# Stage sums behind the next projection, weight transfers later and products in pairs: a hybrid decoder layer on one core of a Trainium2 chip

## The chip, the cores and the metric

The kernel runs on one core of one Trainium2 chip. The metric is the device time of one launch in microseconds. Inputs and outputs lie in the chip's memory; the host only lays the inputs out before the launch.

## What is computed

One layer with two sub-layers, for a sequence of 2048 tokens of width 1024. The part of the reference that matters:

```python
mod = (silu(c) @ w_ada + b_ada)                       # 6 vectors of 1024
sh1, sc1, g1, sh2, sc2, g2 = split(mod, 6)
h = x * (1 + sc1) + sh1
z = h @ w_in                                          # (2048, 1024) @ (1024, 2048)
gate_b, gate_c, v_conv, v_pool = split(z, 4)
y_conv = gate_b * short_conv(gate_c * v_conv, conv_w)  # causal, width 3
y_pool = multiscale_pool(v_pool, w_pool, pool_scale)   # windows 2, 4, 8, 16
mix = concat([y_conv, y_pool]) @ w_out                # (2048, 1024) @ (1024, 1024)
x = layer_norm(alpha * x + (1 + g1) * mix, ln1_g, ln1_b)
h = x * (1 + sc2) + sh2
f = square(relu(h @ w_mlp_in)) @ w_mlp_out            # 1024 -> 4096 -> 1024
x = layer_norm(alpha * x + (1 + g2) * f, ln2_g, ln2_b)
```

All of it is float32.

## The kernel before

**A triple product.** TensorE multiplies in a rounded form of float32. Each operand is split into a high part (a copy in the rounded type, made by ScalarE, L145) and a low part (the operand less its high part, made by VectorE, L146), and `mm3` (L151 to L159) issues three matmuls for one product of tiles: high by high (L152), high by low (L153) and low by high (L154).

**Fewer products.** The large matrix products are cut into 2 by 2 blocks (in the down projection into 4 by 4), and sums of blocks are multiplied instead of the blocks: seven products take the place of eight in the three projections ahead, and the down projection is done in 26 products of such sums. The sums of operands are additions on VectorE (`tt`, L162), and the results are put together by additions out of PSUM.

**Order of the work.** The sequence is done in two halves of 1024 tokens, b = 0 and b = 1. For each half come the input projection (`in_proj_0`, then `in_proj_1` for the second half, four groups of channels), the output projection with the first layer norm (`out_proj`), and the up projection (`first_map`, which runs `up` for g = 0 to 7, eight groups of 512 hidden columns). When both halves are done, `down` computes the down projection for all tokens, and `Close` does the second layer norm and stores the result. Each engine has its own queue and works in order. Which instruction comes next on each queue is set when the kernel is built: the planner takes instructions by the order in which the program names them, but passes over one that would still have to wait in its model. A tile is drawn from a ring of a fixed number of buffers (`o` 10, `r` 5, `w` 6, `h` 28, PSUM banks `ps` 8, `mv` 8), and the next user of a buffer waits for the last reader.

**The up projection's sums.** `up` (L1068) makes four blocks (`c11`, `c12`, `c21`, `c22`) out of seven products, squares them, and then makes sums of them for the down projection, in four stages listed in `U_SUMS`: 3, 7, 13 and 10 additions of 128x256. Sums are stored to `usum` by POOL's DMA queue. For the last group of the first half (`late`), the stages 2 and 3 are put on a list, `owed`. `flush` runs what is on the list. In the kernel before, `flush` is called behind the last product of `up` (L1175, stage 2) and behind product 0 of the next input projection's first group (L744, stage 3).

**The next projection's start.** `group(0)` of `in_proj_1` (L736) runs products 0 to 6 in order. Behind product 0 it copies the banks out (`keep`, ScalarE L730), behind product 1 it adds (`add`, VectorE, from PSUM). Between them `inputs` loads and splits the operands that later products need.

**Transfers beside products.** `sums_down` (L1183) yields 80 DMA transfers of 512 KB, chip memory to chip memory, that make sums of down-projection weights (`wsum`), on POOL's queue; half of them add to what is there. They are tied to products: `mm3` counts its calls while the second half runs (the beats), and at each beat in `W_BEATS` it issues the next transfer, which waits for that product's last matmul. The input projection has the beats 1 to 224, the output projection 225 to 336, the up projection 337 to 784.

**The down projection.** `PRODUCTS` lists 26 products: the slot of `usum`, the weight blocks that are added (most often one or two), a sign, whether new banks are begun, and which results (row block t, column half d) read them. A product that begins no new banks goes on in those of two products before. `operand` loads and splits the operands of a step (a product and a quarter of its depth), four steps ahead. The first two products run their first three quarters before the fourth. When a result has been read for the last time, `finish` multiplies by the gate and adds the residual, and `Close.normalise` follows when both halves of its rows are done. `mv` tiles hold the statistics of rows.

**The gate row.** Beside the second half's up projection, `second_side` runs one job at each of nine beats of its own (`timed`; there are seven to a group from group 1 on, and beat 34 is behind product 0 of group 6). A job runs to its first yield at its beat, and on three beats later. Eight jobs load a column block and form a dot product; the ninth, `gate_row`, adds the bias (L277), then turns eight columns into a row with a transpose on TensorE (L225), a copy on ScalarE (L226) and two DMAs.

**The start of the up projection.** `turned` (L843) stores parts of its operands to `hsave` and loads them again (L880, L895) for sums (`back`). `out_proj` stores normalised rows to `nsave` (L990), on POOL's queue.

Of the kernel before, what the change touches and what calls it, by code (L numbers as in the profile page):

```python
# [27 lines left out]
WINDOWS = (2, 4, 8, 16)  # L28
HALO = 16
Q = 256  # L30
W_BEATS = {*range(48, 200, 7), *range(336, 752, 7)}
QUARTERS = slice(0, 256), slice(256, 512)

SLOTS = 26
# [28 lines left out]
)  # L63
W_KEPT = 18
PRODUCTS = (
# [26 lines left out]
)  # L92
# [15 lines left out]
def tile_hybrid_layer(ctx: ExitStack, tc: tile.TileContext, opening, xT, x, wada, win,  # L108
# [612 lines left out]
    def in_proj_1(X, W, first_w):  # L721
        mixed = []
        ops = Operands(mixed)

        def cut(rows_, h):
            return [r[:, o + h * H : o + h * H + H] for r, o in rows_]

        def keep(dst, banks):
            for p in range(2):
                nc.scalar.copy(dst[p], banks[p])  # L730

        def add(dst, banks):
            for p in range(2):
                tt(dst[p], dst[p], banks[p], ALU.add)

        def group(j):  # L736
            x_, y_, z_ = {}, {}, {}
            ready = W if j == 0 else block_weights(wins[j])
            product = seven(ready, X, None if j else first_w)
            v, u = t_o(WW), t_o(WW)  # L740
            values = (v, HALO), (u, 2)
            product(0, x_, True)
            keep(cut(values, 0), x_)
            flush()  # L744
            nc.vector.tensor_copy(v[:, :HALO], vhalo[:, j, :])
            nc.vector.tensor_copy(u[:, :2], uhalo[:, j, :])
            if j == 0:
                inputs(X, ORDER[3][1])
            product(1, y_, True)
            add(cut(values, 0), y_)  # L750
            if j == 0:
                inputs(X, ORDER[4][1])
            yield
            gc, gb = t_o(), t_o()
            gates = (gc, 0), (gb, 0)
            last = j == NG - 1
            product(2, x_, False)
            keep(cut(values, 1), x_)
            if j == 0:
                inputs(X, ORDER[5][1])  # L760
            product(3, z_, True)
            keep(cut(gates, 1), z_)
            if j == 0:
                inputs(X, ORDER[6][1])
            if last:
                ops.begin(0)
            yield
            product(4, x_, False)
            add(cut(gates, 1), x_)
            if last:  # L770
                ops.begin(1)
            product(5, z_, False)
            add(cut(values, 1), z_)
            if last:
                ops.weights(0, 1)
                pt = pool_mid(1, j, v)
            product(6, x_, False)
            keep(cut(gates, 0), x_)
            if last:
                ops.weights(1, 1)  # L780
                ops.second(0)
            yield
            if not last:
                pt = pool_mid(1, j, v)
            y = gc
            for hs in halves if last else [slice(0, T)]:
                w = hs.stop - hs.start
                tt(u[:, 2 + hs.start : 2 + hs.stop], u[:, 2 + hs.start : 2 + hs.stop], gc[:, hs], ALU.mult)
                conv(j, u[:, hs.start : hs.stop + 2], y[:, hs], w)
                tt(y[:, hs], y[:, hs], gb[:, hs], ALU.mult)  # L790
                if last and hs.start == 0:
                    mixed.extend([y[:, :H], None, pt[:, :H], pt[:, H:]])
                    ops.third(0)
                    ops.third(1)
            sums = mixed_sums(y, pt, u, v)
            if last:
                mixed[1] = sums[0]
                mixed.extend(sums[1:])
            else:
                store_mixed(j, y, pt, u, v)  # L800

        groups = [group(j) for j in range(NG)]
        for _ in range(3):
            next(groups[0])

        for j in range(1, NG):
            last = j == NG - 1
            next(groups[j])
            if not last:
                next(groups[j])  # L810
            next(groups[j - 1], None)
            if last:
                next(groups[j])
            next(groups[j])
        next(groups[-1], None)
        return ops
# [9 lines left out]
        return root  # L826

    def whole_stats(st):
        mv = mk(sm, [P, 8], F32, "mv", 8)
        nc.vector.bn_aggr(mv[:, 0:2], st.rearrange("p a b -> p (a b)"))  # L830
        return mv

# [117 lines left out]
    def out_proj(b, ops):  # L950
# [27 lines left out]

        def end(t, cs, other, scalar=1.0):
            if t not in mv:  # L980
                mv[t] = mk(sm, [P, 8], F32, "mv", 8)
            i = 4 + cs.start // H
            begun[:] = [nc.vector.scalar_tensor_tensor(R[t][:, cs], R[t][:, cs], scalar, other, op0=ALU.mult,
                                                       op1=ALU.add, accum_out=mv[t][:, i : i + 1]).ins]
# [75 lines left out]

    owed = []

    def flush():
        while owed:
            made_of, stage = owed.pop(0)
            made_of(stage)

    def up(b, g, B, beside, turn):  # L1068
# [103 lines left out]
            mark[0] = nc.scalar.activation(c21[:, ps[p]], X[p], AF.Relu).ins  # L1172
        nc.scalar.activation(c21, c21, AF.Square)
        made(c21, 1, 0)
        flush()  # L1175
        if late:
            owed.append((sums, 3))
        else:
# [161 lines left out]
    class Close:  # L1340
# [34 lines left out]
        def add(self, t, cs, ps):  # L1375
# [2 lines left out]
                self.added = tt(F[:, cs], F[:, cs], ps, ALU.add)  # L1378
                return
            if t not in self.mv:  # L1380
                self.mv[t] = mk(sm, [P, 8], F32, "mv", 8)
            i = 4 + cs.start // H
            self.added = nc.vector.scalar_tensor_tensor(F[:, cs], F[:, cs], 1.0, ps, op0=ALU.mult, op1=ALU.add,
                                                        accum_out=self.mv[t][:, i : i + 1])
# [44 lines left out]
        dot(f, r)  # L1429

    def gate_row():
        yield
        biased(G2, G2 + KD)
        g2 = mk(sm, [P, D], F32, "bc", 1)
        row_by_dram(g2, mod[:, G2 : G2 + KD], 1)
        gate.append(g2)

# [13 lines left out]

    def second_side():
        rows_ = [gate_dot(f) for f in range(G2, G2 + KD)] + [gate_row()]
        return timed(dict(zip((4, 6, 11, 13, 18, 20, 25, 27, 31), rows_)))

    gate = []

# [90 lines left out]
```

## Time and profile before

| | |
|---|---|
| median of 3 runs | 1729.69 us (1728.82 to 1731.63) |
| the profiled execution | 1729.34 us, span 1727.6 us |
| mean granted clock of TensorE | 0.993 |
| TensorE busy | 1694.8 us, 98% of the span |
| VectorE busy | 1403.3 us, 81% |
| ScalarE busy | 845.3 us, 49% |
| POOL busy | 378.7 us, 22% |
| memory read and written | 350.01 MB and 159.91 MB |

The time of the profiled execution is that of the launch; the span runs from the first to the last instruction in the trace. Times within the trace are microseconds from the span's start. In the trace the second half's input projection begins near 580 us, its output projection near 742, its up projection near 822 and the down projection near 1148. A line such as `DVE L146` names an engine and the line of the kernel that issued the instruction; a name such as `w<-r,w` gives the tiles written and read, without their numbers. DVE is VectorE, ACT is ScalarE, PE is TensorE and SP the engine that issues most loads.

### The profile page before, as it was taken

The numbers are of one execution on the slowest core, as the hardware profiler recorded it, in microseconds if no ns is written. First come the engines' busy times: TensorE is split into PE (matmuls) and PEld (weight loads), VectorE is DVE, ScalarE is ACT, GpSimd is POOL, SyncE is SP. The second block draws the span as 40 slices with busy tenths as digits, with TensorE's granted clock in tenths as the row PEclk, the third lists the DMA queues.
The fourth block names the chain that finished last, engine by engine and source line by source line (L and its number), as shares of the span: only waits on it lengthen the run. The fifth ranks groups of instructions, "written<-read, shape, count | busy, mean of one in ns | idle before, by whom it ended". The sixth has DMA issues, their size and how long they took to land.

```text
span 1727.6 us, 22038 instructions
## 1 busy us (share of the span) xinstructions
PE 1694.8 (98%) x7519; PEld 1398.3 (81%) x7519; DVE 1403.3 (81%) x2138; ACT 845.3 (49%) x1160; POOL 378.7 (22%) x687
## 2 busy tenths in 40 slices
PE   9999999999999899999999998999999999999998
PEld 8888888878888688888778886878888888888886
DVE  8897798898886766896788787669888867989986
ACT  6323358555555743446655444446543334335553
POOL 0222221344543202201255555540000000000000
PEclk9999999999999999999999999999999999999999
DMA  9998777567764858875899999999999889777772
GB/s 385 348 337 323 300 261 253 192 201 240 241 218 145 258 183 209 250 250 209 276 268 272 269 272 261 259 319 349 336 348 339 339 299 397 285 286 270 276 267 78
DMA packets 149217, 469.47 MB, mean 272 GB/s; under 512 B 20456, under 2 KB 20976, under 8 KB 149104
## 3 DMA queue, kind: packets, MB, share of 16 engines
q1 hardware_dynamic: 93184, 303.38, 49.0%
q0 software_dynamic: 55920, 164.67, 31.9%
q8 instruction: 59, 0.97, 0.2%
q14 instruction: 54, 0.44, 0.1%
HBM read 350.01 MB, written 159.91 MB: 295 GB/s over the span
## 4 chain that ended last, share of the span: by engine, by line
PE 58%; DVE 8%; DMA 7%; issue 6%; ACT 2%; POOL 1%; DVEq 0%; POOLq 0%; SPq 0%; ACTq 0%
PE ps L154 19%; PE ps L153 19%; PE ps L152 19%; DVE o L162 4%; DMA wsum<-in_w 3%; DVE w L146 1%; DVE h L146 1%; DMA o<-hsave 1%; DMA usum<-o 1%; DMA nsave<-o 1%; DMA r<-in_w 0%; DMA r<-winsum 0%; ACT w L145 0%; DMA w<-wsum 0%; DMA r<-in_wins 0%
## 5 line engine op out<-in xcount | busy, mean ns | idle before, releaser
L154 PE MATMUL ps<-h,w 128*128 128x512 f32 x1312 | 512.4, 391 | 11.6 <-DVE w L146 11.5
L152 PE MATMUL ps<-h,w 128*128 128x512 f32 x1312 | 512.7, 391 | 6.8 <-ACT o L1078 3.0
L153 PE MATMUL ps<-h,w 128*128 128x512 f32 x1312 | 512.5, 391 | 1.4 <-DVE h L146 1.2
L153 PE MATMUL ps<-h,h 128*128 128x512 f32 (+1 forms) x1064 | 413.1, 388 | 3.0 <-DVE h L146 3.0
L154 PE MATMUL ps<-h,h 128*128 128x512 f32 (+1 forms) x1064 | 413.2, 388 | 0.0
L152 PE MATMUL ps<-h,h 128*128 128x512 f32 (+1 forms) x1064 | 412.2, 388 | 0.9 <-DVE h L162 0.9
L154 PEld LDWEIGHTS ps<-h,w 128*128 128x128 f32 x1312 | 247.3, 188 | 66.2 <-DVE w L146 14.9
L152 PEld LDWEIGHTS ps<-h,w 128*128 128x128 f32 x1312 | 247.4, 189 | 60.8 <-ACT o L1078 4.3
L1103 POOL DMA_DIRECT2D usum<-o x416 | 229.1, 571 | 286.4 <-DVE o L162 173.7
L153 PEld LDWEIGHTS ps<-h,w 128*128 128x128 f32 x1312 | 247.1, 188 | 54.4 <-DVE h L146 3.1
L145 ACT CAST w<-r 128x1024 fp32r<-128x1024 f32 x156 | 164.1, 1053 | 218.8 <-PE ps L153 194.1
L146 DVE TENSOR_TENSOR w<-r,w 128x1024 fp32r<-128x1024 f32 x156 | 190.0, 1220 | 68.4 <-ACT w L145 67.4
L153 PEld LDWEIGHTS ps<-h,h 128*128 128x128 f32 x1064 | 200.3, 188 | 44.4 <-DVE h L146 3.4
L152 PEld LDWEIGHTS ps<-h,h 128*128 128x128 f32 x1064 | 199.9, 188 | 42.2 <-DVE h L162 1.1
L154 PEld LDWEIGHTS ps<-h,h 128*128 128x128 f32 x1064 | 200.2, 188 | 40.8
L145 ACT CAST h<-r 128x1024 fp32r<-128x1024 f32 (+1 forms) x136 | 136.1, 1007 | 181.0 <-PE ps L153 71.5
L162 DVE TENSOR_TENSOR o<-o,o 128x256 f32<-128x256 f32 (+2 forms) x458 | 200.2, 485 | 10.8 <-DMA o<-hsave 6.1
L146 DVE TENSOR_TENSOR h<-r,h 128x1024 fp32r<-128x1024 f32 (+1 forms) x136 | 157.5, 1165 | 56.8 <-ACT h L145 56.6
L145 ACT CAST h<-w 128x1024 fp32r<-128x1024 f32 x104 | 109.0, 1048 | 100.5 <-DVE w L162 94.9
L162 DVE TENSOR_TENSOR o<-o,ps 128x512 f32<-128x512 f32 x184 | 123.0, 681 | 40.2 <-PE ps L154 38.3
L146 DVE TENSOR_TENSOR h<-w,h 128x1024 fp32r<-128x1024 f32 x104 | 126.8, 1219 | 20.4 <-ACT h L145 20.0
L162 DVE TENSOR_TENSOR o<-o 128x256 f32<-128x256 f32 (+1 forms) x176 | 81.6, 467 | 17.2 <-ACT o L1091 8.7
(166 smaller groups left out, 1423.2 us busy)
## 6 DMA issues: line engine op xcount, KB each, us to landing
usum<-o POOLq DMA_DIRECT2D x416, 128.0 KB, 5.4
r<-usum SPq DMA_DIRECT2D x104, 512.0 KB, 6.1
w<-wsum SPq DMA_DIRECT2D x76, 512.0 KB, 7.3
w<-in_w SPq DMA_DIRECT2D x72, 512.0 KB, 6.8
r<-in_w SPq DMA_DIRECT2D x68, 512.0 KB, 6.8
wsum<-in_w POOLq DMA_DIRECT2D x56, 512.0 KB, 8.6
wsum<-wsum POOLq DMA_DIRECT2D x24, 512.0 KB, 8.0
msum<-o POOLq DMA_DIRECT2D x18, 512.0 KB, 7.1
```

Of the source, the lines that this page charges most:

```text
L145: high = nc.scalar.copy(hi, src)
L146: return high.ins, nc.vector.tensor_tensor(lo, src, hi.bitcast(F32), op=ALU.subtract).ins
L152: nc.tensor.matmul(ps, whi, xhi, start=first, stop=False, skip_group_check=goes_on)
L153: nc.tensor.matmul(ps, whi, xlo, start=False, stop=False, skip_group_check=goes_on)
L154: done = nc.tensor.matmul(ps, wlo, xhi, start=False, stop=last, skip_group_check=goes_on)
L162: return nc.vector.tensor_tensor(out_, a, b_, op=op)
L1103: nc.gpsimd.dma_start(usum[slot, g // 2, :, b, g % 2, :], z)
```

## The change

- `W_BEATS`: the first train of transfers starts at beat 64 instead of 48 and has 21 instead of 22 places; the second starts at 360 instead of 336 and again has 60.
- `PRODUCTS`: the first 24 products change places in pairs (0 with 1, 2 with 3, and so on). The last two stay.
- `flush` takes a number of stages. Its call at the end of `up` is gone. In the next projection's first group, one stage runs behind product 0 and the rest behind product 1's additions.
- `mv` has 12 buffers instead of 8, in three places.
- `gate_row` adds the bias and draws its tile at its own beat and makes the row three beats later; its beat is 33 instead of 31.

```diff
-W_BEATS = {*range(48, 200, 7), *range(336, 752, 7)}
+W_BEATS = {*range(64, 208, 7), *range(360, 776, 7)}
...
 PRODUCTS = (
+    (1, ((2, 1),), 1, True, ((0, 0, -1),)),
     (4, ((13, 1), (14, 1)), -1, True, ((2, 0, -1),)),
-    (1, ((2, 1),), 1, True, ((0, 0, -1),)),
+    (5, ((12, 1),), -1, False, ((0, 1, 1), (2, 1, 1))),
     (6, ((1, 1), (15, -1)), -1, False, ((2, 1, 1),)),
-    (5, ((12, 1),), -1, False, ((0, 1, 1), (2, 1, 1))),
...
+    (17, ((3, 1),), 1, False, ((2, 1, -1),)),
     (25, ((5, 1),), 1, False, ((1, 1, -1),)),
-    (17, ((3, 1),), 1, False, ((2, 1, -1),)),
     (10, ((0, 1),), 1, True, ()),
     (18, ((2, 1),), -1, False, ((2, 0, 1),)),
 )
...
             product(0, x_, True)
             keep(cut(values, 0), x_)
-            flush()
+            if owed:
+                flush(1)
...
             product(1, y_, True)
             add(cut(values, 0), y_)
+            flush()
...
-        mv = mk(sm, [P, 8], F32, "mv", 8)
+        mv = mk(sm, [P, 8], F32, "mv", 12)
...
-    def flush():
-        while owed:
+    def flush(n=4):
+        for _ in owed[:n]:
             made_of, stage = owed.pop(0)
             made_of(stage)
...
         made(c21, 1, 0)
-        flush()
         if late:
             owed.append((sums, 3))
...
     def gate_row():
-        yield
         biased(G2, G2 + KD)
         g2 = mk(sm, [P, D], F32, "bc", 1)
+        yield
         row_by_dram(g2, mod[:, G2 : G2 + KD], 1)
         gate.append(g2)
...
-        return timed(dict(zip((4, 6, 11, 13, 18, 20, 25, 27, 31), rows_)))
+        return timed(dict(zip((4, 6, 11, 13, 18, 20, 25, 27, 33), rows_)))
```

More of the change, by code (lines that the diff above doesn't have):

```diff
@@ L980, in end @@
             if t not in mv:
-                mv[t] = mk(sm, [P, 8], F32, "mv", 8)
+                mv[t] = mk(sm, [P, 8], F32, "mv", 12)
             i = 4 + cs.start // H
@@ L1380, in add @@
             if t not in self.mv:
-                self.mv[t] = mk(sm, [P, 8], F32, "mv", 8)
+                self.mv[t] = mk(sm, [P, 8], F32, "mv", 12)
             i = 4 + cs.start // H
```

18 rows, old and new, of the table PRODUCTS are left out of this document.

## The prediction

> **What bounds the kernel now.** I read the engine table of the page first, then the waits of TensorE, then the stretches around each wait, and last the timelines of those stretches.
>
> ```profile
> PE 1694.8 (98%) x7519; PEld 1398.3 (81%) x7519; DVE 1403.3 (81%) x2138; ACT 845.3 (49%) x1160; POOL 378.7 (22%) x687
> ```
>
> TensorE is busy for 98% of the span, and the change neither adds nor removes a matmul. It can therefore only move the few places where TensorE waits. The waits view of TensorE (what waited, for whom: total us, times, longest) names them.
>
> ```profile
> PE ps L154 <- DVE w L146: 11.5, 5, 6.2
> PE ps L153 <- DVE h L146: 4.2, 3, 3.0
> PE ps L152 <- ACT o L1078: 3.0, 1, 3.0
> PE ps L152 <- DVE o L162: 2.9, 1, 2.9
> ```
>
> L146 is the subtraction on VectorE that makes the low half of an operand, so most of the waiting is for low halves that stand in VectorE's queue. The table by stretches shows what each place costs (stretch, length, busy time and instructions of PE, PEld, DVE, ACT and POOL, granted clock, DMA share, GB/s).
>
> ```profile
> 287.50:327.50 40.00, 40.00 (x178) 32.90 (x177) 38.56 (x52) 26.84 (x32) 4.37 (x9) 1.00 0.41 145
> 840.00:880.00 40.00, 35.68 (x145) 27.50 (x144) 32.12 (x35) 22.43 (x27) 7.63 (x11) 0.96 0.86 259
> 580.00:606.00 26.00, 19.40 (x79) 15.34 (x78) 19.70 (x37) 16.41 (x23) 8.58 (x16) 0.87 0.95 294
> 1062.00:1082.00 20.00, 13.43 (x51) 10.14 (x50) 16.56 (x39) 8.23 (x12) 10.64 (x18) 0.83 1.01 226
> 1148.00:1160.00 12.00, 9.04 (x36) 7.05 (x36) 10.93 (x26) 4.41 (x6) 5.36 (x10) 0.92 1.03 398
> 1130.00:1148.00 18.00, 18.00 (x81) 14.92 (x80) 11.58 (x18) 9.11 (x12) 4.91 (x10) 1.00 0.94 312
> ```
>
> The first row has no wait: 178 matmuls in 40.00 us, 0.2247 us each. By that rate the four others lose 33 x 0.2247 = 7.4 us at 840 to 880, 26 - 79 x 0.2247 = 8.2 at 580 to 606, 20 - 51 x 0.2247 = 8.5 at 1062 to 1082, and 12 - 36 x 0.2247 = 3.9 at 1148 to 1160: 28.0 us together, which is nearly all there is to win. Each loss is the wait and a slow restart behind it, which the clock column shows (0.83 to 0.96).
>
> **Part 1, the gate row (beats 31 to 33, and a yield moved).** In group 6 of the second half's up projection, TensorE's timeline runs:
>
> ```profile
> 1071.46 0.50 PE L152 MATMUL ps<-h,w 128*128 128x512 f32 x1 [3.00 <-ACT o L1078]
> ...
> 1075.77 0.80 PE L154 MATMUL ps<-h,w 128*128 128x512 f32 x1 [3.57 <-DVE w L146]
> 1076.36 0.63 PE L152 MATMUL ps<-h,w 128*128 128x512 f32 x1
> 1076.79 0.63 PE L153 MATMUL ps<-h,w 128*128 128x512 f32 x1
> ...
> 1078.07 0.41 PE L225 MATMUL ps<-ident,mod 128*8 128x128 f32 x1
> ```
>
> VectorE at the same place:
>
> ```profile
> 1065.81 1.22 DVE L146 TENSOR_TENSOR w<-r,w 128x1024 fp32r<-128x1024 f32 x1
> ...
> 1068.45 1.77 DVE L162 TENSOR_TENSOR o<-o,o 128x256 f32<-128x256 f32 x5 [0.17 <-ACT o L1091]
> ...
> 1074.50 1.21 DVE L146 TENSOR_TENSOR w<-r,w 128x1024 fp32r<-128x1024 f32 x1
> ...
> 1081.84 0.69 DVE L162 TENSOR_TENSOR o<-o,ps 128x512 f32<-128x512 f32 x1 [3.24 <-PE ps L154]
> ```
>
> Behind the second wait the matmuls start 0.43 us apart (1076.36, 1076.79), the slow restart. I read the waits themselves as a reordered queue. A matmul that waits for the copy at L1078 writes a bank that product 0 has filled, so it belongs to product 2, not to product 1. Product 1 has had its low half since 1065.81 + 1.22 = 1067.0, yet its first half bank is added only at 1081.84; it stands behind the transpose of L225. That transpose takes its PSUM tile ahead of product 1's and needs mod, which L277 writes in the same beat, so the planner put matmuls of product 2 in front. In the changed kernel mod is written three beats before the transpose, and the transpose stands behind product 2 instead. Product 1 can then run from 1071.46 - 3.00 = 1068.5 to 1068.5 + 24 x 0.2247 = 1073.9. Product 2 starts its two high matmuls (0.45 us) and waits for the low half of 1074.50, ready at 1075.71: 1.4 us are left of the 8.5. I take **-6.7**, allowing 0.4 for the transpose and a short slow restart; bounds -8.5 and 0 (the low half or another bank holds TensorE as long, rival B). The gate row's two DMAs go two beats later on POOL's queue, before store instructions of 0.53 us; nothing needs the row before the down stage.
>
> **Part 2, the transfers 16 beats later.** A beat is a triple product, 3 x 0.2247 = 0.67 us. The first train starts with 48 -> 64; no TensorE wait of the list above lies there, so nothing is won. The second train starts at 360 instead of 336, 16 us later, and that is the start of the second up projection. Here the kernel holds its own control: the first half runs the same stage (287.5 to 327.5) without transfers and loses nothing. The issues of that stage (KB each, median us to landing), second half, then the same stretch of the first half:
>
> ```profile
> nsave<-o POOLq DMA_DIRECT2D x4, 512.0 KB, 13.1
> ...
> o<-hsave SPq DMA_DIRECT2D x2, 512.0 KB, 7.8
> ```
> ```profile
> nsave<-o POOLq DMA_DIRECT2D x4, 512.0 KB, 6.8
> o<-hsave SPq DMA_DIRECT2D x2, 512.0 KB, 5.6
> ```
>
> And the waits of 822 to 880, SP's queue and VectorE, with the first transfer in POOL's timeline:
>
> ```profile
> SPq L880 <- DMA nsave<-o: 6.9, 2, 6.1
> ```
> ```profile
> DVE o L162 <- DMA o<-hsave: 6.1, 3, 4.8
> ```
> ```profile
> 822.48 1.24 POOL L1187 DMA_DIRECT2D wsum<-in_w  x1 [5.41 <-PE ps L154]
> ```
>
> The nsave stores land 6.3 us later beside the transfers, SP's loads of hsave wait 6.9 us for them, VectorE waits 6.1 us for hsave, and its backlog then holds a bank (the 2.9 us wait on L162) and low halves. Without the four transfers before beat 360 the stores go as in the first half; the transfers from 841 on stay. I take **-5.0** of the 7.4, since the second pair of hsave loads still meets them; bounds -7.4 and +3 (the 2.9 us wait again, elsewhere). The Trainium skill, "DMA: Bandwidth & Descriptors", section "Queues, rings and completion order", says that each DMA engine takes its queue rows in turn, packet by packet; the slower landings agree, and by that rule the load is only moved, not removed: rival C below.
>
> **Part 3, the products in pairs.** The down stage now starts with the product of one weight block instead of two summed ones. At its start:
>
> ```profile
> 1149.07 1.23 DVE L162 TENSOR_TENSOR w<-w,w 128x1024 f32<-128x1024 f32 x1 [1.34 <-DMA w<-wsum]
> 1150.21 1.76 DVE L162 TENSOR_TENSOR o<-o,o 128x256 f32<-128x256 f32 x5
> ...
> 1156.25 1.21 DVE L146 TENSOR_TENSOR h<-w,h 128x1024 fp32r<-128x1024 f32 x1
> ```
> ```profile
> 1157.52 0.50 PE L153 MATMUL ps<-h,h 128*128 128x512 f32 x1 [2.96 <-DVE h L146]
> ```
>
> VectorE stood idle 1.34 us for the second of two weight loads, added them (1.23), then ran group 7's sums, and the low half came behind these. With one load per step and no addition, the second step's low half fits ahead of the sums: 3.9 lost, 0.5 left, **-3.4**; bounds -3.9 and +1.2 (one more subtraction behind the sums). By the Trainium skill, "TensorE: Matmul & The Clock Gate", part 1, a gap under about 3.4 us needn't drop the clock; the trace disagrees (0.92 behind 2.96 us), and by the page this term would be nearer -2.5. Later, row block t=1 is finished one product later. VectorE has room for that in the last product; bounds 0 and +1, taken 0:
>
> ```profile
> 1702.57 0.69 DVE L1383 SCALAR_TENSOR_TENSOR h<-h,ps 128x512 f32<-128x512 f32 x1 [6.82 <-PE ps L154]
> ```
>
> **Part 4, the sums behind the next two products.** Stage 2 is 13 and stage 3 is 10 additions of 128x256. TensorE's wait and the queue ahead of it:
>
> ```profile
> 590.71 0.75 DVE L162 TENSOR_TENSOR o<-o,o 128x256 f32<-128x256 f32 x2
> ...
> 593.99 0.68 DVE L162 TENSOR_TENSOR o<-o,ps 128x512 f32<-128x512 f32 x1
> ...
> 595.26 2.35 DVE L146 TENSOR_TENSOR h<-r,h 128x1024 fp32r<-128x1024 f32 x2
> 597.53 1.21 DVE L146 TENSOR_TENSOR w<-r,w 128x1024 fp32r<-128x1024 f32 x1
> ```
> ```profile
> 598.79 0.79 PE L154 MATMUL ps<-h,w 128*128 128x512 f32 x1 [6.20 <-DVE w L146]
> ```
>
> The low half that TensorE waits for is product 2's. In the new text stage 3 still stands before product 2 and before the inputs split at 595.26; only product 1's additions from PSUM (593.99) come ahead of it now, and stage 2 passes nothing that runs on VectorE. So I expect nearly the same queue: **0**. Bounds: -8.2 (the wait goes) and +2 (five additions, 5 x 0.34 from 590.71 with two in 0.75, fall behind 593.99). The mv tiles, 12 instead of 8, cost nothing: they run no instruction.
>
> **The other end of the trains.** The last transfer moves from beat 735 to 766; five come later than any did.
>
> ```profile
> L1244 SPq DMA_DIRECT2D w<-wsum x6: 319/320/424, 1137.1 to 1146.6; - x6
> L1187 POOL DMA_DIRECT2D wsum<-in_w x3: 941/943/977, 1108.0 to 1124.9; - x3
> ```
>
> They now run into the loads that start the down stage at 1137.1, in a stretch with 0.94 of the DMA taken. Each moves 0.5 MB in and 0.5 out, 3.4 us at 312 GB/s. Queued behind them on POOL are group 7's usum stores, which the order of steps (the fourth quarter last) needs only from the seventh step on. I take **+0.6**, bounds 0 and 12 (5 x 3.4 less the 5 us of three loads saved in part 3).
>
> **The sum.** -6.7 - 5.0 - 3.4 + 0 + 0.6 = -14.5 on the profiled execution's 1729.34 us (span 1727.6), which is within 0.4 of the runs' median of 1729.69: **1715 us**.
>
> **Rivals.** A: stage sums leave product 2's low half in front, and the wait at 598.79 goes too: 1715 - 8 = 1707. For it speaks that all 10 additions of stage 3 stand directly before it; against it that they still do in the text. B: the gate row's gain is eaten, because the low half at 1074.50 is late whatever the order, or another bank is held: 1715 + 6.7 = 1722. For it: VectorE works without a gap from 1068.45 to 1075.7. C, on the slower side: the transfers' load only moves. The trains' end falls on groups 6 and 7 and the down stage; the loads there come 12 us late, and the low halves of the last groups as late as at 840 to 880 (7.4). That decides once the first operands of the down stage are held up by more than the 5 us that their saved loads give. With parts 2 and 3 lost: 1729.3 - 6.7 + 12 + 7.4 = 1742. For it: DMA shares of 0.94 to 1.03 from 1062 on; against: the first step now needs half the weight loads. D: the planner's order gives back what it takes, no change: 1729.
>
> **How the numbers follow.** Forecast 0.45, A 0.13, B 0.22, C 0.15, D 0.05. About 0.2%, 3.5 us, is what a measurement of this kernel can tell from no change. Faster: 0.45 + 0.13 + 0.22 = 0.80; same 0.05; slower 0.15. The range takes in A's end and D and leaves out C: 1706 to 1731.
>
> **What would show it.** Right: no wait over 2 us on PE around the L225 transpose, and L225 behind product 2; nsave landing near 7 us and no DVE wait over 1 us for hsave; no wait in the first steps of the down stage; the 6 us wait on L146 at the second input projection still there. Wrong: new waits on L1244 operands after 1148, or a long wait in groups 3 to 7.

## The result and the profile after

The changed kernel takes 1728.09 us (median of 12 runs, 1726.51 to 1729.70) where the kernel before, run beside it, takes 1729.84 (1727.14 to 1732.46). The ratio is 0.9989, 95% interval 0.998 to 0.9998: by the bound of 0.2% no change; the interval stays below 1, but the 1.75 us gained lie within the 3.5 us that the prediction counts as no change. The forecast was 1715. The profiled execution took 1726.58 us, with a span of 1724.7 against 1727.6 before.

In the changed kernel the lines from L745 on stand one or two higher than before: the copy that was L1078 is L1080, a usum store L1105, a wsum transfer L1188, the down stage's loads L1242 (usum) and L1245 (weights), the scaling of the residual rows L1194 and L1195.

The engine table and the waits of TensorE:

```profile
PE 1692.8 (98%) x7519; PEld 1399.9 (81%) x7519; DVE 1402.6 (81%) x2138; ACT 844.1 (49%) x1160; POOL 377.9 (22%) x687
```
```profile
PE ps L154 <- DVE w L146: 12.9, 5, 5.4
PE ps L153 <- DVE h L146: 8.4, 1, 8.4
```

TensorE still waits for the same thing, low halves from L146. Two of the waits of before (3.0 for the copy, 2.9 for L162) are gone, and one wait of 8.4 has come. The table by stretches shows where (columns as in the prediction):

```profile
580.00:606.00 26.00, 20.61 (x79) 16.49 (x78) 21.05 (x38) 19.00 (x25) 8.60 (x16) 0.87 0.94 305
840.00:880.00 40.00, 40.00 (x178) 32.95 (x177) 38.57 (x56) 26.62 (x31) 11.51 (x18) 1.00 0.88 245
906.00:922.00 16.00, 13.83 (x60) 10.80 (x59) 13.72 (x23) 7.55 (x9) 9.21 (x17) 1.00 1.00 282
1056.00:1076.00 20.00, 20.00 (x90) 16.47 (x89) 18.54 (x39) 12.12 (x16) 10.93 (x21) 1.00 0.99 268
1104.00:1120.00 16.00, 11.41 (x44) 8.92 (x43) 8.18 (x15) 2.36 (x3) 9.61 (x18) 0.89 0.89 277
1152.00:1172.00 20.00, 12.53 (x49) 10.24 (x50) 14.64 (x19) 8.00 (x9) 8.07 (x15) 0.83 1.02 362
```

At 0.2247 us a matmul, the second and fourth rows now lose nothing (7.4 and 8.5 before), and the first loses what it did (8.2). New losses stand in group 2 (16 - 60 x 0.2247 = 2.5), in group 7 (6.1) and at the start of the down stage (9.0, where the row before lost 3.9).

The same as a lead: how much earlier than in the kernel before a stretch begins (start of its first L152 matmul in TensorE's timeline; us, minus is later; groups of the second half's up projection; "step 5" is the fifth operand of the down stage, behind which the lead stays as it is). The other kernels of this document stand below it.

| kernel | group 0 | 2 | 6 | 7 | down | step 5 |
|---|---|---|---|---|---|---|
| changed | 1.6 | 8.5 | 6.2 | 15.1 | 8.6 | 2.9 |
| e1_old_beats | 0.7 | 3.2 | 1.4 | 8.4 | 0.3 | -2.9 |
| e2_new_beats | -0.2 | 6.6 | 3.0 | 5.7 | 3.3 | -2.3 |
| e3_old_products | -0.2 | 6.7 | 2.9 | 11.4 | 1.0 | -5.1 |
| e4_gate | 0.8 | 0.5 | -3.0 | 4.1 | -0.9 | -2.4 |
| e5_out_proj | -4.2 | 1.2 | -2.6 | 6.3 | 6.3 | 2.0 |
| e7_gate_split | -1.9 | 5.4 | 4.3 | 13.2 | 11.1 | 4.0 |
| e10_out_proj_rows | -6.9 | -1.5 | -6.9 | 2.0 | 2.0 | 6.9 |
| e11_together | -0.3 | 6.4 | 2.2 | 11.0 | 11.0 | 15.9 |

The first row is the whole result: the two gains were made (1.6 to 8.5 by group 2, 6.2 to 15.1 in group 6) and given back, 6.5 in group 7 and 5.7 at the start of the down stage. Single values shift from run to run: e7 has the changed kernel's text up to group 0 and stands 3.5 us behind it there (-1.9 against 1.6). So the steps along a row count, and not its values alone.

Where it was given back, TensorE's and VectorE's timelines run:

```profile
1110.98 0.50 PE L154 MATMUL ps<-h,w 128*128 128x512 f32 x1 [4.59 <-DVE w L146]
...
1159.47 0.80 PE L153 MATMUL ps<-h,h 128*128 128x512 f32 x1 [8.41 <-DVE h L146]
```
```profile
1099.79 2.77 DVE L162 TENSOR_TENSOR o<-o,o 128x256 f32<-128x256 f32 x8
1108.36 0.76 DVE L162 TENSOR_TENSOR o<-o,o 128x256 f32<-128x256 f32 x2 [5.81 <-DMA usum<-o]
...
1109.71 1.22 DVE L146 TENSOR_TENSOR w<-r,w 128x1024 fp32r<-128x1024 f32 x1
...
1154.71 0.76 DVE L162 TENSOR_TENSOR o<-o,o 128x256 f32<-128x256 f32 x2 [6.31 <-DMA usum<-o]
...
1158.20 1.22 DVE L146 TENSOR_TENSOR h<-w,h 128x1024 fp32r<-128x1024 f32 x1
```

Read the bracket of the second row: an addition that reads and writes only tiles waits 5.81 us for a DMA, and for one that takes data out of a tile (usum<-o, a store). The sums of the stages write into cells whose earlier content is still being stored, so the addition may not start before that store has landed. The low half stands behind it in VectorE's queue. POOL's timeline tells why the stores are late:

```profile
1093.59 0.55 POOL L228 DMA_DIRECT2D bc<-grow  x1 [5.65 <-DMA grow<-tmp]
1094.96 1.86 POOL L1188 DMA_DIRECT2D wsum<-in_w  x2 [0.82 <-PE ps L153]
1096.14 1.26 POOL L1188 DMA_DIRECT2D wsum<-wsum  x1
1096.72 3.38 POOL L1105 DMA_DIRECT2D usum<-o  x5
...
1131.11 1.81 POOL L1188 DMA_DIRECT2D wsum<-in_w  x2 [0.75 <-DMA usum<-o]
1135.99 0.59 POOL L1105 DMA_DIRECT2D usum<-o  x1 [3.07 <-DMA wsum<-in_w]
...
1143.97 0.54 POOL L1105 DMA_DIRECT2D usum<-o  x1 [3.01 <-DMA wsum<-in_w]
1149.03 0.54 POOL L1105 DMA_DIRECT2D usum<-o  x1 [4.52 <-DMA wsum<-in_w]
1154.09 0.54 POOL L1105 DMA_DIRECT2D usum<-o  x1 [4.52 <-DMA wsum<-in_w]
```

First the gate row's second DMA holds POOL 5.65 us for the landing of its first, and three transfers and five stores go out in one bunch behind it. Later four stores are issued only when a transfer before them has landed; what makes POOL wait for that landing no run shows.

The kernel before has the gate row's hold too, but at another place among the sums. Its hold on POOL, the first addition of group 6's stage 1 on its VectorE, and the same addition in the changed kernel:

```profile
1093.12 0.56 POOL L228 DMA_DIRECT2D bc<-grow  x1 [5.38 <-DMA grow<-tmp]
```
```profile
1102.57 0.42 DVE L162 TENSOR_TENSOR o<-o 128x256 f32<-128x256 f32 x1
```
```profile
1091.84 0.42 DVE L162 TENSOR_TENSOR o<-o 128x256 f32<-128x256 f32 x1
```

Before, the hold ends 9.5 us ahead of that stage; in the changed kernel the stage begins 1.8 us before the hold ends, and its stores queue behind it.

Two groups of lines, transfers (L1188, from 1090 to 1160) and stores (L1105, from 1094 to 1160), sum it up:

```profile
  POOL usum L1105: 15.1, 4
...
DMA to landing us min/median/max: 4.2/11.5/21.9
```
```profile
  DVE o L162: 12.1, 2
...
DMA to landing us min/median/max: 3.2/7.5/19.2
```

In the first, "who waited for it": the stores waited 15.1 us for transfers, which took up to 21.9 us to land. In the second, VectorE waited 12.1 us for stores. I call this theory T: late transfers delay stores, stores hold the in-place sums, the sums hold the low half.

### The profile page after: what moved, and what is told of

Same layout as the page of the kernel before. It is cut to its first block, busy times and chain, and to the rows that moved or that the text cites. A ratio compares the mean times of both kernels' runs of the same rounds, so it can differ in the third digit from the quotient of the medians.

```text
span 1724.7 us, 22033 instructions
## 1 busy us (share of the span) xinstructions
PE 1692.8 (98%) x7519; PEld 1399.9 (81%) x7519; DVE 1402.6 (81%) x2138; ACT 844.1 (49%) x1160; POOL 377.9 (22%) x687
## 5 line engine op out<-in xcount | busy, mean ns | idle before, releaser
L152 PE MATMUL ps<-h,w 128*128 128x512 f32 x1312 | 512.4, 391 | 1.0 <-ACT w L145 0.9
L152 PE MATMUL ps<-h,h 128*128 128x512 f32 (+1 forms) x1064 | 413.1, 388 | 0.9 <-DVE h L162 0.9
L152 PEld LDWEIGHTS ps<-h,w 128*128 128x128 f32 x1312 | 247.2, 189 | 54.0 <-ACT w L145 2.3
L1105 POOL DMA_DIRECT2D usum<-o x416 | 226.0, 555 | 271.9 <-DVE o L162 147.5
L146 DVE TENSOR_TENSOR w<-r,w 128x1024 fp32r<-128x1024 f32 x156 | 189.9, 1220 | 69.2 <-ACT w L145 68.1
L152 PEld LDWEIGHTS ps<-h,h 128*128 128x128 f32 x1064 | 200.2, 188 | 42.0 <-DVE h L162 1.1
L162 DVE TENSOR_TENSOR o<-o,o 128x256 f32<-128x256 f32 (+2 forms) x458 | 201.0, 486 | 20.7 <-DMA usum<-o 18.6
L146 DVE TENSOR_TENSOR h<-r,h 128x1024 fp32r<-128x1024 f32 (+1 forms) x136 | 157.4, 1164 | 65.5 <-ACT h L145 65.1
L146 DVE TENSOR_TENSOR h<-w,h 128x1024 fp32r<-128x1024 f32 x104 | 126.7, 1218 | 25.0 <-ACT h L145 24.8
L162 DVE TENSOR_TENSOR o<-o,ps 128x512 f32<-128x512 f32 x184 | 122.4, 681 | 29.2 <-PE ps L154 27.6
L162 DVE TENSOR_TENSOR o<-o 128x256 f32<-128x256 f32 (+1 forms) x176 | 81.8, 468 | 17.6 <-ACT o L1093 8.8
```

What stands on the lines that cost most here:

```text
L146: return high.ins, nc.vector.tensor_tensor(lo, src, hi.bitcast(F32), op=ALU.subtract).ins
L152: nc.tensor.matmul(ps, whi, xhi, start=first, stop=False, skip_group_check=goes_on)
L162: return nc.vector.tensor_tensor(out_, a, b_, op=op)
L1105: nc.gpsimd.dma_start(usum[slot, g // 2, :, b, g % 2, :], z)
```

## The experiments

**One part put back or done alone.** e1: the changed kernel with the old beats. e2: the kernel before with the new beats. e3: the changed kernel with the old `PRODUCTS`. e4: the kernel before with the gate row's change.

```diff
 e1: -W_BEATS = {*range(64, 208, 7), *range(360, 776, 7)}
     +W_BEATS = {*range(48, 200, 7), *range(336, 752, 7)}
 e4: -        yield
             biased(G2, G2 + KD)
             g2 = mk(sm, [P, D], F32, "bc", 1)
     +        yield
     ... 25, 27, 31)  ->  ... 25, 27, 33)
```

> The changed kernel with the old beats of both trains (48 to 199 and 336 to 751); everything else as changed. Theory T (late transfers delay the usum stores on POOL's queue, VectorE's in-place sums wait for these stores to land, and the low half behind them is late): the loss of about 7 us at 840 to 880 comes back, and the waits at group 7 (4.6) and at the start of the down stage (8.4) shrink to 0 to 3 each; about 1724 us. Theory U (the new product order itself makes the start of the down stage late): the 8.4 us wait stays, and with the loss at 840 to 880 back the time is about 1735 us.

> The kernel before with the new beats alone. Theory T: it gains about 7 us by group 2 of the second half and gives most of it back: the wait at the start of the down stage grows from 3.0 to 6 to 9 us, perhaps with a wait in group 7; about 1726 to 1729 us. Theory U: the gain stays, and the wait at the start of the down stage stays near 3 us; about 1722 us.

> The changed kernel with the old order of products. Theory T: the start of the down stage waits as long as in the changed kernel, 8 us give or take 2; 1726 to 1730 us. Theory U: the wait goes back to about 3 us; about 1722 us.

> The kernel before with the gate row's change alone (mod written at beat 33, the transpose and its two DMAs at beat 36). Theory T: the stall of 8.5 us around the transpose goes, group 7 starts 6 to 9 us earlier than before, and with the old beats only 0 to 3 us are lost again at group 7 and at the start of the down stage; 1721 to 1724 us. Theory V (the gate row's late DMAs alone hold POOL's queue and so the stores): a wait of 3 to 5 us in group 7 as in the changed kernel, and about 1727 us.

Measured: 1732.71, 1731.62, 1733.01 and 1732.29 us beside 1732.13 for the kernel before; ratios 1.0011 (1.0001 to 1.0022), 1.0000 (0.9988 to 1.0012), 1.0007 (0.9998 to 1.0016), 1.0004 (0.9996 to 1.0013). No part brings anything by itself, though the table of leads shows each gain where it was forecast: 6.8 us by group 2 in e2, 7.1 in group 6 in e4. For e1 and e4 theory T forecast 1724 and 1721 to 1724, and missed: with the old beats the lead is given back too. Its times for e2 and e3 were missed as well, by 2.6 and 3.0 us (the kernel before ran 2.3 us slower here than beside the changed kernel). U falls: in e3, with the old order, the first steps of the down stage wait 8.3 us in three waits, where the changed kernel waits 8.4 in one, and the kernel is not faster but slower. V has something: POOL stood 5.34 us for the gate row's first DMA in e4, and in e1, with the transfers at their old beats, an addition in group 7 still waits 5.01 us for a store. And e1 shows a bound that I had not had on the list, ScalarE at the start of the down stage:

```profile
1163.34 1.06 ACT L1194 ACTIVATE o<-o 128x1024 f32<-128x1024 f32 x1 [10.18 <-DMA o<-in_rows]
```
```profile
1168.17 0.49 PE L152 MATMUL ps<-h,h 128*128 128x512 f32 x1 [3.95 <-ACT h L145]
```

The scaling of a residual row waits in ScalarE's queue for its 0.5 MB load, and the copy that makes the next operand stands behind it. So at least three things end at nearly the same time: stores behind transfers, the gate row's hold on POOL, the rows. The next runs take them away one by one.

**The transfers moved ahead.** e5: 15 transfers of the second train go into the second out-projection. e6: the first train is denser.

```diff
 e5: +W_BEATS = {*range(64, 208, 7), *range(232, 334, 7), *range(360, 664, 7)}
 e6: +W_BEATS = {*range(64, 208, 4), *range(360, 664, 7)}
```

> The changed kernel with 15 of the second train's transfers moved ahead into the second out-projection (beats 232 to 330, where the profile of the changed kernel shows DMA shares of 0.71 and 0.50); the second train then ends at beat 661, not 766, so groups 6 and 7 and the start of the down stage run without transfers. Theory T (the transfers at the end delay the usum stores, and VectorE's in-place sums wait for these): the waits of 4.6 us in group 7 and 8.4 us at the start of the down stage shrink to 0 to 2 us each, and a lead of 8 to 15 us on the kernel before lasts to the end: 1714 to 1720 us, up to 5 more if the loads of the out-projection come late. Theory V (VectorE's own backlog and the gate row make these waits, the transfers do not): both waits stay, 1726 to 1730 us.

> The changed kernel with the first train at every fourth beat instead of every seventh (36 transfers in beats 64 to 204) and the second train ending at beat 661. Theory T: as with the transfers in the out-projection, the two late waits shrink to 0 to 2 us each, 1714 to 1722 us; the second input projection, with a DMA share of 0.50 to 0.95 there, may lose some us of it. Theory V: both waits stay, 1726 to 1730 us.

Measured: 1728.08 and 1727.69 us, ratios 0.9982 (0.997 to 0.9995) and 0.9983 (0.9972 to 0.9995) to the kernel before. Both times missed T's forecasts and lie in V's range of 1726 to 1730; the place in group 7 fits T, and not V, by which both waits stay. In e5 the wait in group 7 is gone, no addition waits for a store there, and the stores land in:

```profile
DMA to landing us min/median/max: 2.0/4.0/8.9
```

Two things ate the gain. The out-projection paid for the transfers (1.0 us of lead at its start, -4.2 at group 0), and at the start of the down stage the rows came last, as in e1:

```profile
1157.59 1.06 ACT L1194 ACTIVATE o<-o 128x1024 f32<-128x1024 f32 x1 [12.03 <-DMA o<-in_rows]
```
```profile
1163.83 0.79 PE L152 MATMUL ps<-h,h 128*128 128x512 f32 x1 [5.57 <-ACT h L145]
```

e6 went the same way: its denser train cost the second input projection 4.6 us of lead (-1.3 to -5.9), and the down stage waited 3.06 and 0.77 us.

**POOL and its queue.** e7: the gate row's second DMA comes three beats behind its first, and the bias goes back to beat 31. e8: SP, not POOL, issues the usum stores of groups 6 and 7.

```diff
 e7: ...
     +        nc.gpsimd.dma_start(grow[1].rearrange("(k p) -> k p", k=KD), r[:KD, :P])
     +        yield
     +        nc.gpsimd.dma_start(g2, grow[1].partition_broadcast(P))
     ...
 e8: -            nc.gpsimd.dma_start(usum[slot, g // 2, :, b, g % 2, :], z)
     +            queue = nc.sync if b and g >= 6 else nc.gpsimd
     +            queue.dma_start(usum[slot, g // 2, :, b, g % 2, :], z)
```

> The changed kernel with the gate row's two DMAs three beats apart (mod at beat 31, transpose and first DMA at beat 36, second DMA at beat 39), so that POOL does not stand 5.65 us for the first to land. If this hold on POOL is what makes the stores late: the wait of 4.6 us in group 7 falls to 0 to 2, and the down stage's 8.4 falls too; 1721 to 1725 us. If the transfers behind it are, wherever they are issued: the wait in group 7 moves to the start of the down stage or stays, 1726 to 1730 us.

> The changed kernel with the usum stores of groups 6 and 7 of the second half issued by SP, not by POOL, so that they stand behind no transfer in a queue. If the order within POOL's queue delays the stores: they land within some 5 us of their issue, and the two late waits shrink to 0 to 3 us each; 1716 to 1722 us, or more where SP's loads now stand behind them. If the rate of the 16 DMA engines does it, whatever the queue: the landings stay at 8 to 18 us and so do the waits, 1726 to 1732 us.

e7: 1726.16 us, ratio 0.9969 (0.9959 to 0.9979), about 3.5 us better than the changed kernel's 0.9989 (the two were not measured side by side). The wait of 4.59 in group 7 became one of 1.70 for a copy, and the lead at the down stage is 11.1 instead of 8.6; there it is lost again, to a wait of 8.06. There an addition waits 5.44 us for a store. So the hold costs time by itself, and with the late transfers left in place the gain is mostly lost again at the down stage.

e8: 1741.92 us, ratio 1.0062 (1.0045 to 1.0079). On SP's queue the stores landed no sooner in the median (9.5 us, 7.5 in the changed kernel), though at worst in 11.5 us against 19.2, and SP now waits for the sums before it may issue the loads behind them. SP's waits from 1080 to 1160, and ScalarE's:

```profile
SPq L1106 <- DVE o L162: 37.0, 14, 23.8
```
```profile
1134.33 1.04 ACT L145 CAST h<-r 128x1024 fp32r<-128x1024 f32 x1 [20.23 <-DMA r<-usum]
```

This run says that a store on another queue is no faster in the median while the DMA is full; whether the order in POOL's queue costs anything beside that it cannot tell, since it hurt the loads.

**The rows later, and everything together.** e9: the changed kernel with the rows' work from the fourth product on. e10: e5 with the same. e11: a first train that is dense only where the DMA was half idle (share 0.50 at 620 to 660 in the changed kernel), a second train that ends at beat 710, the rows later, the gate row split as in e7.

```diff
 e9, e10, e11: -            if n > 0 and gp % 2 == 0:
               +            if n > 2 and gp % 2 == 0:
 e11: +W_BEATS = {*range(56, 120, 4), *range(120, 208, 7), *range(360, 717, 7)}
```

> The changed kernel with the residual rows' work, which begins with two broadcast loads of 0.5 MB and their scaling on ScalarE, started at the fourth product of the down stage and not at the second. Theory T (at the start of the down stage VectorE waits for stores behind late transfers): these loads are a second bound beside the stores, not the last one; the wait of 8.4 us shrinks by 0 to 2 us, 1725 to 1729 us. Theory R (the row loads and ScalarE's wait of 12.4 us for them make the start of the down stage late): the wait goes, 1719 to 1722 us.

> The kernel with 15 transfers in the second out-projection, and the row loads started at the fourth product as well. Where the transfers no longer run in groups 6 and 7, VectorE did not wait for stores, and ScalarE's 12.0 and 3.1 us for the rows came last at the start of the down stage. So its wait of 5.6 us there falls to 0 to 2 us, and the lead of 6.3 us over the kernel before lasts: 1721 to 1725 us. If the operands are late for the DMA rate alone, whatever is put off: 5 us of wait stay, 1727 to 1729 us.

> The changed kernel with the first train at every fourth beat from 56 to 116 and every seventh from 120 (29 transfers, most of the added ones where the DMA share was 0.50), the second train ending at beat 710, the row loads at the fourth product, and the gate row's second DMA three beats later. By theory T with the rows as second bound: no wait over 2 us in group 7 and at the start of the down stage, a lead of 10 to 15 us to the end, 1714 to 1720 us. If the waits only move again: 1725 to 1729 us.

e9: 1729.88 us (T: 1725 to 1729), ratio 0.9989 (0.9979 to 0.9998), that of the changed kernel. The rows alone gain nothing, since the stores are still there; VectorE and TensorE:

```profile
1159.80 0.76 DVE L162 TENSOR_TENSOR o<-o,o 128x256 f32<-128x256 f32 x2 [5.13 <-DMA usum<-o]
```
```profile
1164.56 0.80 PE L153 MATMUL ps<-h,h 128*128 128x512 f32 x1 [7.27 <-DVE h L146]
```

e10: 1721.15 us, ratio 0.9938 (0.9922 to 0.9954). With the stores early, the same edit takes the wait of 5.57 away altogether; it gains 7 us on e5 (1728.08). e11: 1712.67 us (1712.05 to 1713.41), ratio 0.9894 (0.9878 to 0.9909), which beats both kernels. Its stretch from group 7 into the down stage, and all the larger waits that TensorE has left:

```profile
1094.00:1172.00 78.00, 78.00 (x346) 64.61 (x345) 63.70 (x104) 43.81 (x50) 26.25 (x49) 1.00 0.97 304
```
```profile
PE ps L154 <- DVE w L146: 9.5, 3, 6.1
PE ps L152 <- ACT w L145: 2.2, 2, 1.2
```

TensorE runs 78 us without a gap, at a DMA share of 0.97. The DMA is as full as before (0.98 in the kernel before and 0.99 in the changed one over the same stretch), and the stores land in 6.9 us in the median, against 7.5 in the changed kernel, and in 9.6 against 19.2 at worst. What changed is that POOL waits for no transfer before it issues a store, and no addition waits for a store. T with the rows as second bound is shown by this row of three: stores alone (e5) 0.9982, rows alone (e9) 0.9989, both (e10) 0.9938.

**The sums alone** (part 4), the kernel before with the two flushes moved (stage 2 goes behind product 0 and stage 3 behind product 1, as in the changed kernel; the expectation names the stages otherwise):

> The kernel before with the change of the sums alone (the last group's stages 0 to 2 behind product 1 of the second input projection, not behind product 6 of the group and product 0). By the reading of the trace the wait of about 6 us at the second input projection stays and nothing else changes: 1728 to 1731 us. If the additions that come behind product 1 hold VectorE there: the wait grows by up to 2 us, 1731 us; if the low half comes ahead of them: it goes, 1722 us.

1732.57 us, ratio 1.0009 (0.9999 to 1.0019): nothing gained, the wait at the second input projection stays (5.93).

**What each part is worth once the waits behind it are gone.** Each kernel is e11 with one edit: the old order of products (e13), the old gate row (e14), stage 3 put behind product 2 of the input projection (e15), the gate row as in the changed kernel, not split (e16).

> The kernel of all measures together (1712.7 us), with the old order of products. With the stores and the rows out of the way this shows what the pairs change by themselves. By the prediction's third part (one weight load and no addition in the first steps): a wait of 3 us comes back at the start of the down stage, 1715 to 1717 us. If the first operands are early enough either way: 1712 to 1714 us.

> The kernel of all measures together (1712.7 us), with the gate row as it was before the change (mod and transpose in one beat). By the prediction's first part: the stall of 7 to 9 us around the transpose comes back in group 6 and nothing behind gives it back, 1719 to 1722 us. If the lead there is made up elsewhere, as in the changed kernel: 1712 to 1715 us.

> The kernel of all measures together (1712.7 us), with the last group's stage 3 put behind product 2 of the second input projection and not behind product 1. If the low half of product 2 is late because stage 3 stands before it in VectorE's queue: the wait of 6.1 us at 599 us goes with its slow restart, 1704 to 1708 us. If its operands are late for another reason (loads at a DMA share of 0.8 to 0.95, or tiles that the sums hold longer): 1711 to 1718 us.

> The kernel of all measures together (1712.7 us), with the gate row's two DMAs in one beat as in the changed kernel. If POOL's wait of some 5 us for the first of them costs time only where transfers are queued behind it: the second train has ended by then, and the time stays at 1712 to 1714 us. If it delays the usum stores of group 7 enough by itself: a wait of 2 to 4 us in group 7, 1715 to 1718 us.

Measured beside 1732.04 for the kernel before; e11 was not measured beside these, so I compare ratios, with e11's 0.9894 (0.9878 to 0.9909):

| kernel | us | ratio | against e11 |
|---|---|---|---|
| e13_old_products | 1716.20 | 0.9909 (0.9894 to 0.9923) | +2.6 us |
| e14_old_gate | 1717.40 | 0.9916 (0.9901 to 0.9931) | +3.8 us |
| e15_sums_later | 1710.42 | 0.9877 (0.9862 to 0.9892) | -2.9 us |
| e16_no_split | 1717.04 | 0.9912 (0.9896 to 0.9929) | +3.1 us |

The last column is the difference of ratios times 1732; the intervals overlap with e11's, so the timelines decide. e13 and e16 came out within one of their two forecasts; e14 and e15 lie between theirs. TensorE in e13, in e14, in e16 and in e15:

```profile
1144.04 0.50 PE L153 MATMUL ps<-h,h 128*128 128x512 f32 x1 [2.55 <-DVE h L146]
```
```profile
1068.26 0.80 PE L154 MATMUL ps<-h,w 128*128 128x512 f32 x1 [3.57 <-DVE w L146]
```
```profile
1111.64 0.79 PE L154 MATMUL ps<-h,w 128*128 128x512 f32 x1 [3.96 <-DVE w L146]
```
```profile
602.49 0.80 PE L152 MATMUL ps<-h,w 128*128 128x512 f32 x1 [4.60 <-ACT w L145]
```

e13 brings back the wait of the kernel before at the start of the down stage, e14 the stall at the transpose. e16 waits in group 7 as the changed kernel does, though its second train is 56 beats shorter. POOL in e16, and the same transfers in e11:

```profile
1095.89 0.55 POOL L228 DMA_DIRECT2D bc<-grow  x1 [6.24 <-DMA grow<-tmp]
1096.43 1.90 POOL L1188 DMA_DIRECT2D wsum<-in_w  x2
1097.60 3.97 POOL L1105 DMA_DIRECT2D usum<-o  x6
```
```profile
1090.56 1.28 POOL L1188 DMA_DIRECT2D wsum<-in_w  x1
1092.65 0.90 POOL L1188 DMA_DIRECT2D wsum<-in_w  x1 [0.81 <-DMA wsum<-in_w]
```

The last two transfers stand behind the hold, leave 4 to 6 us later than in e11, and take six stores with them; VectorE then waits 6.17 us for a store. So the gate row's change as it was made is worth 1717.40 - 1717.04 = 0.4 us, which is no difference: it takes a stall from group 6 and makes one in group 7. Split, it is worth 3.8 by the ratios.

Four of the kernels sort VectorE's waits for a store (those over 2 us from group 6's sums on) by the two causes:

| kernel | last transfer at beat | gate row's two DMAs | wait in group 7 | wait at the down stage |
|---|---|---|---|---|
| changed | 766 | together | 5.81 | 6.31 |
| e7_gate_split | 766 | apart | none | 5.44 |
| e16_no_split | 710 | together | 6.17 | none |
| e11_together | 710 | apart | none | none |

The wait in group 7 goes with the hold, the one at the down stage with the late transfers. The hold needs transfers beside it: in e5, with the DMAs together and the last transfer at beat 661, neither wait is there. The later rows, which e11 and e16 also have, take neither away (e9: 7.46 and 5.13).

In e15 the wait of 6.13 for the low half of product 2 goes, and one of 4.60 for a high half comes one product later; with 1710.42 us this is the fastest kernel of the study. So stage 3 in front of it did hold that low half (rival A's condition, which the change as made does not meet), and the next bound lies close behind.

## Why the prediction was wrong

The forecast was 14.5 us faster on the profiled execution; it was 2.8 (1729.34 to 1726.58).

- **Part 1, right where it looked, and wrong beyond it.** The stall at the transpose went; L225 stands between the last matmul of product 2 and the first of product 3, and neither waits:

```profile
1072.76 0.39 PE L154 MATMUL ps<-h,w 128*128 128x512 f32 x1
1072.99 0.27 PE L225 MATMUL ps<-ident,mod 128*8 128x128 f32 x1
1073.02 0.48 PE L152 MATMUL ps<-h,w 128*128 128x512 f32 x1
```

  The lead grew by 8.9 us in group 6 (6.7 forecast). The step that failed is "The gate row's two DMAs go two beats later on POOL's queue, before store instructions of 0.53 us". I priced the DMAs that stand behind by the time of their instruction, and not by the wait of the second DMA for the first, which holds POOL 5.65 us. The kernel before has this hold as well (5.38 us), ahead of group 6's sums; the gained lead and the two later beats put it in front of their stores. e14 and e16 show that this costs what the part gains.
- **Part 2, right.** In the stretch 820 to 862 the nsave stores land in 6.9 us (median), the hsave loads in 5.7, no VectorE wait for hsave is left in the list of waits, and the loss at 840 to 880 is 0:

```profile
nsave<-o POOLq DMA_DIRECT2D x4, 512.0 KB, 6.9
o<-hsave SPq DMA_DIRECT2D x4, 512.0 KB, 5.7
```

  The lead grew by 6.9 (5.0 forecast), of which 2.4 goes again in group 2, where an addition waits for a store behind a transfer in the same way.
- **Part 3, right in size, its place taken.** In e13 against e11 the pairs are worth 2.6 us by the ratios, whose intervals overlap; 3.4 was forecast, and the wait of 2.55 in e13 is none in e11. In the changed kernel the start of the down stage shows none of it (8.4 us of waits, 8.3 in e3 with the old order), because the low half now waits behind sums that wait for stores. e3 is slower than the changed kernel by 3 us all the same (1.0007 against 0.9989), and gives back 10.4 in group 7 where that gives back 6.5; why, the runs leave open.
- **Part 4, right.** 0 forecast; e12 shows none, and the wait at the input projection stayed at 5.4 us.
- **The other end of the trains, wrong, and it decides the case.** I took +0.6 with bounds of 0 and 12; the leads given back in group 7 and at the down stage are 6.5 + 5.7 = 12.2. That the bound of 12 fits is luck: it was worked out from transfers that make the down stage's loads late, and the 12.2 contains the gate row's hold (e7 gives back 2.1 in group 7). The step that failed is "Queued behind them on POOL are group 7's usum stores, which the order of steps (the fourth quarter last) needs only from the seventh step on". I asked who reads the stored data, and not who waits to overwrite the tile that the store reads. That is an addition of one of the next stages, which stands in VectorE's queue ahead of the low half.
- **The rivals.** C named the right place and the right resource, but not the mechanism (operands of the down stage 12 us late) nor its size: it counted part 2 as lost, but parts 1 and 2 were both gained first, so the time came out at no change and not at 1742. D, at 0.05, had the right time, but not by the planner's order, so that was luck; and that the measured time lies within 1706 to 1731 is owed to D's end of the range, not to the sum.

## What to carry to other kernels

When a transfer is moved later, ask of every DMA behind it both who reads its result and who waits to reuse its source: a store that nobody reads for long can still hold the next instruction that writes its tile. A DMA that waits for another DMA holds its queue for the landing, not for its own 0.5 us; put something between the two. And where several waits end at one place, taking away the one in front shows little: e5 and e9 each gained next to nothing over the changed kernel (ratios 0.9982 and 0.9989 to its 0.9989), their two edits together 9 us (0.9938).

## What the runs showed of the hardware

- **Landings went with the load more than with the size.** From 1094 to 1160, usum stores of 128 KB on POOL's queue and usum loads of 512 KB on SP's landed in 4.0 and 4.6 us (medians) in e5, at a DMA share of 0.73. In the changed kernel, at a share of 0.99, they took 7.5 and 8.5, and the slowest store 19.2.
- **The clock dropped behind some short gaps and not behind others.** In the changed kernel the wait of 2.13 us in group 2 left the clock at 1.00 (row 906 to 922 above). Behind a wait of 2.08 us in e12, and behind the 2.55 us of e13, the rows of their stretches read 0.83:

```profile
852.00:862.00 10.00, 7.92 (x28) 5.79 (x27) 9.26 (x10) 7.75 (x8) 1.53 (x2) 0.83 0.30 93
```
```profile
1140.00:1150.00 10.00, 7.45 (x26) 5.67 (x25) 10.00 (x19) 3.84 (x5) 4.99 (x10) 0.83 1.03 331
```

  The Trainium skill, "TensorE: Matmul & The Clock Gate", part 1, gives an idle window of about 3.4 us that runs freely and does not reset when a kernel starts. That gaps of nearly the same length fall either way agrees with a free-running window; a drop behind 2.08 us does not agree with a gap of a full window being needed.
